# A two-layer encoder on one core: up-products turned weight-stationary, and sums of down weights made ahead through HBM

## The chip, the cores and the metric

The kernel runs on one core of a Trainium2 chip. The metric is the device time in microseconds from start to end; lower is better. The profile is one execution with every instruction recorded.

## What is computed

A trunk of two layers over 256 tokens of width 2048, all in float32. Layer 0 mixes tokens with a bidirectional mLSTM, layer 1 with a bidirectional HGRN2; each mixer is followed by a gated feed-forward block (ConvGLU). The change lies in the feed-forward blocks:

```python
def conv_glu(hn, w_up, conv_w, conv_b, w_down):
    u = hn @ w_up                          # (256, 2048) @ (2048, 2 * 5504)
    a, v = jnp.split(u, 2, axis=-1)
    ...
    c = conv_b
    for j in range(CONV_W):                # width 3 along the tokens
        c = c + ap[:, j:j + s] * conv_w[j]
    return (jax.nn.gelu(c, approximate=False) * v) @ w_down   # (256, 5504) @ (5504, 2048)

for layer in range(DEPTH):
    hn = rmsnorm(h, norm_mix_g[layer])
    h = h + (mlstm_mixer(hn, ...) if layer % 2 == 0 else hgrn_mixer(hn, ...))
    h = h + conv_glu(rmsnorm(h, norm_ffn_g[layer]), ...)
return rmsnorm(h, final_g)
```

## The kernel before

Every matrix product is made of three: activations and weights are each split into a high part (cast to fp32r) and a low remainder, and high x high, high x low and low x high are added up in PSUM. The weights stream from HBM in 1 MB pieces into three buffers tagged `raw`, on SP's queue. `halves` splits a piece: ScalarE casts 1024 columns into `wh`, VectorE subtracts to get `wl` (four buffers each). `split_weights` and `split_pair` are generators of such pieces; `stream` pulls them three ahead of the products that use them.

Three forms of product occur. A `Chunk` of kind `tm` (token-major) holds the activations stationary and streams 512 weight columns, 6 matmuls for each 128 rows of weights. A `Chunk` of kind `fm` (feature-major) holds a weight block stationary: for each 128 rows and each of two 128-column blocks, `wh` against the 512 columns of high and low activations (line 388), then `wl` against the 256 columns of high ones (line 391). With `turns` set, at k = 1 both `wh` passes run first and then both `wl` passes (lines 380 and 382). A `Pair` makes two 512-column output blocks at once, for both halves of the tokens: its unit is a *couple* of two 128-row blocks of weights, which the plan marks by a letter. An `N` couple takes 8 products of three 512-column matmuls; an `S` couple takes 7, as in Strassen's scheme with Winograd's sums, and an `H` is half an `N`. An `S` needs sums of the four weight blocks (`T4`, three subtractions by VectorE, lines 237 to 240), which are split like weights, and sums of the four activation blocks (`forms`, line 399). After the last `S` of a pair, `middle` puts the scheme's accumulators together (`combine`, line 1104) and adds them; `done` adds the rest when the pair is through.

In a feed-forward block the 43 tiles of 128 hidden features are taken in three parts of 16, 16 and 11. For each part, the up products of its tiles run first and then the down products with its features, added into `hm`. Up products go by `Pair`, four tiles of a and v at a time (`UP_PLAN` with three couples of eight by seven; `UP_LAST`, for a part's last group, with two). Their outputs are token-major, so the side job `raise_up` turns each tile by four TensorE transposes (line 1069), convolves, applies Gelu and the gate, splits the result into `g`, and makes the forms that the down pair will need. Down products go by two `Pair`s for each part (`DOWN_PLAN`: two couples of eight by seven for 16 tiles, one for 11); in the last part of layer 1 the second pair is replaced by two `tm` chunks.

The order of the work between matmuls is set by `Side`: side jobs are generators, moved on by `tick` with a written-out estimate of the time that each group of matmuls takes. Within what the dependencies allow, a list scheduler orders the instructions of each engine. A queue is in order once written.

Of the kernel before, what the change touches and what calls it, by code (L numbers as in the profile page):

```python
# [15 lines left out]
P = 128  # L16
T = 256
# [4 lines left out]
GROUP = 4  # L22
UP_PLAN = "SNSNSNNN"
UP_LAST = "SNSNNNNN"
PACE = 2.5
PACE_LAST = 0.8
DOWN_PLAN = {16: "SNSNNNNN", 11: "SNNNNH"}
# [36 lines left out]
def trunk_kernel(ctx, tc, xT, x_d, fg_d, pp_d, cst_d, sel_d, w_gate, w_first, w_aq, w_ak, w_av, w_ao, w_aout,  # L64
                 w_bq, w_bv, w_bg, w_bout, w_up, w_down, w_last, out, mscr):
# [30 lines left out]
    class Side:  # L96
        def __init__(self):
            self.now, self.jobs, self.turned = 0.0, [], False
# [16 lines left out]
        def until(self, ready):  # L115
            while not ready():
                assert self.jobs
                for job in list(self.jobs):
                    self.step(job)

# [102 lines left out]

    def split_pair(ch):
        w, b0 = ch.w, 0
        for kind in ch.plan:
            n = (2 if kind == "H" else 4) * w
            raw = wpool.tile([P, 2048], F32, tag="raw", bufs=RAW, name="raw")
            nc.sync.dma_start(raw[:, :n], ch.src[:, b0:b0 + n])
            b0 += n  # L230
# [4 lines left out]
            T4 = ch.pool().tile([P, 2048], F32, tag="T4", bufs=1, name="T4")  # L235
            b12 = raw[:, 0:w].unsqueeze(1).broadcast_to([P, 2, w])
            dve.tensor_tensor(T4[:, 0:2 * w].rearrange("p (a b) -> p a b", a=2), b12,  # L237
                              raw[:, w:3 * w].rearrange("p (a b) -> p a b", a=2), ALU.subtract)
            dve.tensor_tensor(T4[:, 2 * w:3 * w], raw[:, 2 * w:3 * w], T4[:, 0:w], ALU.subtract)
            dve.tensor_tensor(T4[:, 3 * w:4 * w], raw[:, 3 * w:4 * w], T4[:, 2 * w:3 * w], ALU.subtract)  # L240
# [5 lines left out]
    def stream_pair(ch, take):  # L246
# [18 lines left out]
        left, k = ch.plan.count("S"), 0  # L265
        for c, kind in enumerate(ch.plan):
            end = c == len(ch.plan) - 1
            if kind == "S":
# [3 lines left out]
                F, fin = ch.form(c), left == 0  # L272
# [30 lines left out]
            D = ch.form(c) if left else None  # L303
# [95 lines left out]
    def forms(x2, kind, mp, tag, fe):  # L399

        n = 4 if kind == "S" else 2
        e = fe.tile([P, 512], F32, tag="fe", bufs=1, name="fe")
# [13 lines left out]
    def wanted(plan):  # L416
        last = plan.rfind("S")
        return {c: k for c, k in enumerate(plan) if c <= last}
# [118 lines left out]
    class FinalNorm:  # L537

        def begin(self, mp):
            self.mp = mp  # L540
            self.g = mp.tile([P, D], F32, name="fg")
# [495 lines left out]
    def ffn(layer, norm, nxt):  # L1037
# [5 lines left out]
        def begin():  # L1043
            box["mp"] = stack.enter_context(tc.tile_pool(name="ff", bufs=1))
            box["mp"].tile([P, LEAD], F32, name="lead")
            box["xf"] = tc.tile_pool(name="xf", bufs=1)
            box["xp"] = box["xf"].__enter__()
        norm.pool, norm.temps = lambda: box.get("xp"), lambda: box["mp"]

        def end():  # L1050
            box["xf"].__exit__(None, None, None)
            if last:
                nxt.begin(stack.enter_context(tc.tile_pool(name="fin", bufs=1)))

        def raise_up(st):
            while not st["ready"]:
                yield 0.5
            at, w = st["at"], st["w"]
            mp = box["mp"]
            for j in range(w // P):  # L1060
                f, i = st["f"] + j, st["i"] + j
                if i % 2 == 0:
                    st["GT"].c2 = mp.tile([P, 2, T], F32, tag="c2", bufs=2, name="c2")
                c = st["GT"].c2[:, i % 2]
                pt = aux("pt")
                for n in range(2):
                    for t in range(2):
                        o = n * T + t * P
                        pe.transpose(pt[:, o:o + P], at[:, t, n * 512 + j * P:n * 512 + (j + 1) * P], ident)  # L1069
                cw = [col("conv_w", (layer * 3 + k) * FT + f) for k in range(3)]  # L1070
                act.activation(c, pt[:, 0:T], AF.Identity, scale=cw[1], bias=col("conv_b", layer * FT + f))
                dve.scalar_tensor_tensor(c[:, 1:T], pt[:, 0:T - 1], cw[0], c[:, 1:T], ALU.mult, ALU.add)
                dve.scalar_tensor_tensor(c[:, 0:T - 1], pt[:, 1:T], cw[2], c[:, 0:T - 1], ALU.mult, ALU.add)
                act.activation(c, c, AF.Gelu)
                dve.tensor_tensor(c, c, pt[:, T:2 * T], ALU.mult)
                g = slot(i, "g")
                act.copy(g[:, 0:T], c)
                dve.tensor_tensor(g[:, T:2 * T], c, g[:, 0:T].bitcast(F32), ALU.subtract)
                st["GT"].x[i] = g
                if i % 2 and i // 2 in st["GT"].want:  # L1080
                    st["GT"].forms[i // 2] = forms(st["GT"].c2, st["GT"].want[i // 2], mp, f"gf{i // 2}", mp)
                yield PACE_LAST if st['end'] else PACE
            st["over"] = True

        class Gated:
            def __init__(self, nf):
                self.x, self.forms, self.want = [None] * nf, {}, wanted(DOWN_PLAN[nf])

            def get(self, k):
                side.until(lambda: self.x[k] is not None)  # L1090
                return self.x[k]

            def form(self, c):
                side.until(lambda: c in self.forms)
                return self.forms[c]

        def room(st):
            side.until(lambda: all("over" in o for o in st["wait"]))
            st["at"] = box["mp"].tile([P, 2, 1024], F32, tag="at", bufs=1, name="at")

        def rows(d, w):
            return d.rearrange("p (n c) -> p n c", n=2)[:, :, 0:w]
# [12 lines left out]
        before = None  # L1115
        for part, (f0, nf) in enumerate(PARTS):
            GT = Gated(nf)
            for i in range(0, nf, GROUP):
                w = min(GROUP, nf - i) * P
                st = dict(f=f0 + i, i=i, GT=GT, w=w, end=i + GROUP >= nf, wait=[before] if before else [])  # L1120
                before = st

                def middle(acc, st=st):
                    room(st)
                    at, w, rc = st["at"], st["w"], norm.rc
                    combine(acc, at, w)
                    for t in range(2):
                        v = rows(at[:, t], w)
                        act.activation(v, v, AF.Copy, scale=rc[:, t:t + 1])

                def done(acc, st=st):
                    w = st["w"]
                    plain = "at" not in st
                    if plain:
                        room(st)
                    for t in range(2):
                        d, v, sc = rows(acc["rows"][t], w), rows(st["at"][:, t], w), norm.rc[:, t:t + 1]
                        if plain:
                            act.activation(v, d, AF.Copy, scale=sc)
                        else:  # L1140
                            dve.scalar_tensor_tensor(v, d, sc, v, ALU.mult, ALU.add)
                    st["ready"] = True
                st["ready"] = False
                ch = Pair(w_up[layer, (f0 + i) // GROUP], UP_LAST if i + GROUP >= nf else UP_PLAN, norm.x, norm.form, lambda acc, done=done, st=st: (done(acc), side.push(raise_up(st))),
# [161 lines left out]
```

## Time and profile before

| | |
|---|---|
| median of 3 runs | 2405.66 us (2405.57 to 2408.1) |
| the profiled execution | 2404.82 us, its span 2403.0 us |
| TensorE matmul busy | 2389.1 us, 99% of the span |
| VectorE busy | 2017.9 us, 84% |
| ScalarE busy | 1396.5 us, 58% |
| GpSimd busy | 163.6 us, 7% |
| granted TensorE clock | 0.999 of full speed |
| moved by DMA | 451.01 MB, mean 188 GB/s |

The span runs from the first to the last instruction. A busy share is the time in which the engine had an instruction under way; a busy TensorE need not be at its peak, since matmuls are pipelined and one that takes 0.39 us from start to end is followed by the next after some 0.23. In the profile, PE is TensorE's matmul, PEld its weight load, DVE is VectorE, ACT is ScalarE, POOL is GpSimd and SP the engine that issues the weight DMAs. L255 is line 255 of the kernel. A row of a group of instructions gives count, busy time and mean duration, then the idle time of the engine just before them and what ended it.

### The profile page before, as it was taken

How to read it: one execution, taken by the hardware profiler on the slowest of the kernel's cores; microseconds unless marked ns; L12 is line 12 of the kernel's file. 1: busy time of each engine (PE TensorE's matmuls, PEld its weight loads, DVE VectorE, ACT ScalarE, POOL GpSimd, SP SyncE). 2: the span in 40 equal slices, each digit the busy share in tenths (PEclk: the TensorE clock that was granted, in tenths of full speed). 3: DMA queues.
4: the chain of work that ended last, by engine and by line, in shares of the span. 5: the costliest groups of instructions: out<-in, count | busy, mean ns of one | idle time of the engine just before them, and what ended most of it. 6: DMA issues, size and time to landing. Idle time of an engine off the chain costs nothing.

```text
span 2403.0 us, 34456 instructions
## 1 busy us (share of the span) xinstructions
PE 2389.1 (99%) x13165; PEld 1997.6 (83%) x13165; DVE 2017.9 (84%) x3009; ACT 1396.5 (58%) x2063; POOL 163.6 (7%) x223
## 2 busy tenths in 40 slices
PE   9999999999999999999999999999999999999998
PEld 8888888788887888888888888888878888888897
DVE  7766667998889887997888888886898889988896
ACT  6655465666456555665555555556566556654664
POOL 0100000000000000001222222220000000000000
PEclk9999999999999999999999999999999999999999
DMA  7654554555555556455554555545556555555564
GB/s 295 203 179 170 186 175 175 195 185 198 193 192 193 193 193 210 163 200 182 176 169 167 173 176 168 169 174 178 191 175 210 177 208 193 186 196 195 191 210 143
DMA packets 67061, 451.01 MB, mean 188 GB/s; under 512 B 7744, under 2 KB 8384, under 8 KB 15440
## 3 DMA queue, kind: packets, MB, share of 16 engines
q1 hardware_dynamic: 64800, 442.32, 53.1%
q0 software_dynamic: 1232, 5.31, 1.0%
q8 instruction: 103, 1.69, 0.3%
q10 hardware_dynamic: 864, 1.19, 0.1%
q14 instruction: 62, 0.51, 0.1%
HBM read 446.62 MB, written 2.16 MB: 187 GB/s over the span
## 4 chain that ended last, share of the span: by engine, by line
PE 91%; DVE 7%; issue 1%; ACT 1%; DMA 0%; SPq 0%; POOLq 0%; POOL 0%; ACTq 0%; DVEq 0%
PE c L255 44%; PE mm L388 9%; PE mm L371 7%; PE mm L372 7%; PE mm L373 7%; PE m L255 5%; PE mm L391 4%; DVE wl L162 3%; PE pt L1069 1%; PE mm L380 1%; PE pn L737 1%; PE pd L920 1%; PE py L969 1%; DVE T L237 1%; PE pz L482 0%
## 5 line engine op out<-in xcount | busy, mean ns | idle before, releaser
L161 ACT CAST wh<-raw 128x1024 fp32r<-128x1024 f32 (+1 forms) x837 | 829.1, 1001 | 563.0 <-PE c L255 220.9
L162 DVE TENSOR_TENSOR wl<-raw,wh 128x1024 fp32r<-128x1024 f32 (+1 forms) x837 | 967.5, 1167 | 224.1 <-ACT wh L161 223.3
L255 PE MATMUL c<-wh,xt 128*128 128x512 f32 (+1 forms) x1944 | 620.1, 386 | 0.0
L255 PEld LDWEIGHTS c<-wh,xt 128*128 128x128 f32 x1944 | 363.8, 188 | 71.3 <-ACT wh L161 4.8
L255 PE MATMUL c<-wl,xt 128*128 128x512 f32 (+1 forms) x972 | 374.9, 386 | 0.0
L388 PE MATMUL mm<-xt,wh 128*128 128x512 f32 x940 | 331.9, 396 | 0.0
L255 PE MATMUL c<-wh,g 128*128 128x512 f32 x1028 | 325.3, 390 | 0.0
L161 ACT CAST wh<-T 128x1024 fp32r<-128x1024 f32 (+1 forms) x158 | 161.2, 1038 | 186.7 <-PE c L255 154.6
L391 PE MATMUL mm<-xt,wl 128*128 128x256 f32 x940 | 264.3, 281 | 0.0
L255 PEld LDWEIGHTS c<-wh,g 128*128 128x128 f32 x1028 | 192.8, 188 | 41.2 <-ACT wh L161 1.2
L255 PEld LDWEIGHTS c<-wl,xt 128*128 128x128 f32 x972 | 182.5, 188 | 39.3 <-DVE wl L162 5.1
L162 DVE TENSOR_TENSOR wl<-T,wh 128x1024 fp32r<-128x1024 f32 (+1 forms) x158 | 188.1, 1206 | 31.2 <-ACT wh L161 22.8
L388 PEld LDWEIGHTS mm<-xt,wh 128*128 128x128 f32 x940 | 176.4, 188 | 38.7
L255 PE MATMUL c<-wl,g 128*128 128x512 f32 x514 | 200.8, 391 | 0.0
L255 PE MATMUL c<-wh,F 128*128 128x512 f32 (+1 forms) x500 | 196.0, 395 | 0.8 <-ACT wh L161 0.8
L371 PE MATMUL mm<-wh,xt 128*128 128x512 f32 x480 | 188.2, 392 | 0.0
L372 PE MATMUL mm<-wl,xt 128*128 128x512 f32 x480 | 187.7, 391 | 0.0
L373 PE MATMUL mm<-wh,xt 128*128 128x512 f32 x480 | 187.3, 390 | 0.0
L391 PEld LDWEIGHTS mm<-xt,wl 128*128 128x128 f32 x940 | 177.0, 188 | 0.8
L255 PE MATMUL m<-wh,F 128*128 128x512 f32 (+1 forms) x316 | 116.9, 395 | 0.0
L255 PEld LDWEIGHTS c<-wl,g 128*128 128x128 f32 x514 | 96.5, 188 | 21.3 <-DVE wl L162 1.4
L255 PEld LDWEIGHTS c<-wh,F 128*128 128x128 f32 x500 | 94.0, 188 | 20.2 <-ACT wh L161 1.6
(272 smaller groups left out, 3399.4 us busy)
## 6 DMA issues: line engine op xcount, KB each, us to landing
raw<-in_w_up SPq DMA_DIRECT2D x160, 1024.0 KB, 4.8
raw<-in_w_down SPq DMA_DIRECT2D x79, 1024.0 KB, 4.9
raw<-in_w_bq SPq DMA_DIRECT2D x48, 1024.0 KB, 5.1
raw<-in_w_ao SPq DMA_DIRECT2D x16, 1024.0 KB, 4.8
raw<-in_w_aout SPq DMA_DIRECT2D x16, 1024.0 KB, 4.8
raw<-in_w_bv SPq DMA_DIRECT2D x16, 1024.0 KB, 4.8
raw<-in_w_bg SPq DMA_DIRECT2D x16, 1024.0 KB, 4.8
raw<-in_w_bout SPq DMA_DIRECT2D x16, 1024.0 KB, 4.8
```

The source lines that it names most:

```text
L161: act.copy(wh[:, :m], r)
L162: dve.tensor_tensor(wl[:, :m], r, wh[:, :m].bitcast(F32), ALU.subtract)
L237: dve.tensor_tensor(T4[:, 0:2 * w].rearrange("p (a b) -> p a b", a=2), b12, raw[:, w:3 * w].rearrange("p (a b) -> p a b", a=2), ALU.subtract)
L255: pe.matmul(acc[name][:, 0:w], a, b, start=name not in begun, stop=sp and i == 2)
L371: pe.matmul(ps[t], xh, wh[:, c], start=st, stop=False)
L372: pe.matmul(ps[t], xh, wl[:, c], start=False, stop=False)
L373: pe.matmul(ps[t], xl, wh[:, c], start=False, stop=sp)
L380: pe.matmul(ps[f], wh[:, cs[f]], x, start=st, stop=False)
L388: pe.matmul(ps[f], wh[:, c:c + P], x, start=st, stop=False)
L391: pe.matmul(ps[f][:, 0:T], wl[:, c:c + P], x[:, 0:T], start=False, stop=sp)
L737: pe.matmul(pn[:, 0:258], w, v, start=(i == 0), stop=(i == len(parts) - 1))
L920: pe.matmul(pd[o:o + w, c:c + w], k[:, b * w:(b + 1) * w], q[:, e * w:(e + 1) * w], start=True, stop=True)
```

## The change

- Up products: each tile's a and v is one `fm` chunk of 256 columns (`w_up` is laid out anew for it), normalised by `fm_scaled` and convolved straight from PSUM in `done_up`. There are no couples by seven in the ups any more, no transposes of the result, no `raise_up`, no `at` tile, and no forms of the norm's output. Only the first chunk of each part has `turns`.
- Down pairs: five of eight couples go by seven, and two of five and a half in an 11-tile part (both pairs of a part have the same plan). The letter `P` is an `S` whose weight sums come ready and split from HBM: `split_pair` loads three of its four raw blocks and then the sums, 2 MB in four loads on GpSimd's queue.
- These sums are made by the side job `sums_ahead` during the ups of the same part: two half couples (256 of 512 columns each) for each `P`, one every 12 ticks; load on SP's queue, three subtractions, cast and remainder, then two stores on GpSimd's queue into the new HBM tensor `sums`. Four spare tiles `pr0` to `pr3` serve both the making and the loading.
- The down pair's combining tile now comes from the three `raw` buffers; the last norm's gain tile shares `T4`'s place and is loaded when the last down pair ends.

```diff
-UP_PLAN = "SNSNSNNN"
-UP_LAST = "SNSNNNNN"
-DOWN_PLAN = {16: "SNSNNNNN", 11: "SNNNNH"}
+TURNS = 1
+A = "PSNSPSNN"
+B = "PSNNNH"
+DOWN_PLAN = {16: A, 11: B}
+REST = 8.0
+EACH = 12.0
...
+    def pair_sums(b, t):
+        dve.tensor_tensor(t[:, 0:2], b[:, 0:1].broadcast_to(b[:, 0:2].shape), b[:, 1:3], ALU.subtract)
+        dve.tensor_tensor(t[:, 2], b[:, 2], t[:, 0], ALU.subtract)
+        dve.tensor_tensor(t[:, 3], b[:, 3], t[:, 2], ALU.subtract)
+    def sums_ahead(srcs, box):
+        yield REST
+        due, h = side.now, 256
+        for n, src in srcs:
+            for o in (0, h):
+                while side.now < due and not side.flush:
+                    yield 0.1
+                due += EACH
+                b, t, th, tl = (spare(i, box) for i in range(4))
...
+                nc.sync.dma_start(b, src.rearrange("p (a b) -> p a b", a=4)[:, :, o:o + h])
+                pair_sums(b, t)
+                act.copy(th, t)
+                dve.tensor_tensor(tl, t, th.bitcast(F32), ALU.subtract)
+                for j, v in enumerate((th, tl)):
+                    pool.dma_start(sums[n, j]...[:, :, o:o + h], v...)
+            stored.append(n)
     def split_pair(ch):
...
+            skip = w if kind == "P" else 0
+            nc.sync.dma_start(raw[:, skip:n], ch.src[:, b0 + skip:b0 + n])
+            if kind == "P":
+                yield halves(raw[:, w:3 * w], 2 * w)
+                yield halves(raw[:, 3 * w:4 * w], w)
+                n = ch.made[c]
+                side.until(lambda: n in stored)
+                for i in range(2):
+                    z = [spare(2 * i + j, ch.box) for j in range(2)]
+                    for j in range(2):
+                        pool.dma_start(z[j], sums[n, j][:, 1024 * i:1024 * i + 1024])
+                    yield z
+                continue
...
-        def raise_up(st):
...
+        def done_up(f, i, GT):
+            def go(ps):
...
+                fm_scaled(ps[0], R, a)
+                fm_scaled(ps[1], R, v)
+                act.activation(c, a, AF.Identity, scale=cw[1], bias=col("conv_b", layer * FT + f))
+                dve.scalar_tensor_tensor(c[:, 1:T], a[:, 0:T - 1], cw[0], c[:, 1:T], ALU.mult, ALU.add)
+                dve.scalar_tensor_tensor(c[:, 0:T - 1], a[:, 1:T], cw[2], c[:, 0:T - 1], ALU.mult, ALU.add)
+                act.activation(c, c, AF.Gelu)
+                dve.tensor_tensor(c, c, v, ALU.mult)
+                g = slot(i, "g", mp)
+                act.copy(g[:, 0:T], c)
+                dve.tensor_tensor(g[:, T:2 * T], c, g[:, 0:T].bitcast(F32), ALU.subtract)
...
...
         for part, (f0, nf) in enumerate(PARTS):
-            for i in range(0, nf, GROUP):
-                ch = Pair(w_up[layer, (f0 + i) // GROUP], UP_LAST if i + GROUP >= nf else UP_PLAN, norm.x, norm.form, ..., middle, w=w)
+            for i in range(nf):
+                chunks.append(Chunk("fm", w_up[layer, f0 + i], KT, norm.x, done_up(f0 + i, i, GT), turns=1 if i < TURNS else 0))
+                chunks[-1].apart = bool(part) and i == 0
...
-                    room(before)
-                    combine(acc, before["at"], 512)
+                    at = wpool.tile([P, 2048], F32, tag="raw", bufs=RAW, name="at")...
+                    combine(acc, at, 512)
...
-    n0, n1, n2, n3 = Norm("mix_g", 0), Norm("ffn_g", 0, UP_PLAN), Norm("mix_g", KT), Norm("ffn_g", KT, UP_PLAN)
+    n0, n1, n2, n3 = Norm("mix_g", 0), Norm("ffn_g", 0), Norm("mix_g", KT), Norm("ffn_g", KT)
+    sums = nc.dram_tensor("sums", (count, 2, P, 2048), F32R, kind="Internal").ap()
```

More of the change, by code (lines that the diff above doesn't have):

```diff
@@ L271, in stream_pair @@
                 left -= 1
[L272 removed]
+                F, fin = ch.form(c, kind), left == 0
                 def form(i):
@@ L1089, in get, with form @@
             def get(self, k):
-                side.until(lambda: self.x[k] is not None)
                 return self.x[k]
[L1093 to L1102, printed above, removed]
+            def form(self, c, kind):
+                return self.forms[c, kind]
@@ L1113, in combine @@
                               v5.unsqueeze(1).broadcast_to([P, 2, w]), ALU.add)
-        before = None
         for part, (f0, nf) in enumerate(PARTS):
             GT = Gated(nf)
-            for i in range(0, nf, GROUP):
[L1119 to L1144, printed above, removed]
-                          middle, w=w)
-                ch.pool = lambda: box["mp"]
-                chunks.append(ch)
-            before = dict(wait=[before], over=True)
-            final = last and part == len(PARTS) - 1
@@ L1182, in ffn @@
         return chunks, begin, stack.close
+    numbers = list(range(sums.shape[0]))
     pool.memset(ones, 1.0)
```

130 lines of the change are left out of this document (68 added, 62 removed).

## The prediction

> **What bounds the kernel now.** I read the page first (busy shares, chain), then the two feed-forward stretches cut at their stage boundaries, then in a down stage VectorE's groups and the waits, and the DMA issues last.
>
> ```profile
> span 2403.0 us, 34456 instructions
> PE 2389.1 (99%) x13165; PEld 1997.6 (83%) x13165; DVE 2017.9 (84%) x3009; ACT 1396.5 (58%) x2063; POOL 163.6 (7%) x223
> ...
> DMA  7654554555555556455554555545556555555564
> GB/s 295 203 179 170 186 175 175 195 185 198 193 192 193 193 193 210 163 200 182 176 169 167 173 176 168 169 174 178 191 175 210 177 208 193 186 196 195 191 210 143
> ...
> PE 91%; DVE 7%; issue 1%; ACT 1%; DMA 0%; SPq 0%; POOLq 0%; POOL 0%; ACTq 0%; DVEq 0%
> ```
>
> (The two rows in the middle are the DMA share and the GB/s in 40 slices.) TensorE is 91% of the chain and busy 99% of the span, so a change pays only by shortening TensorE's own stream, and costs wherever the stream is starved. VectorE, at 84%, is next. Stage by stage (columns: stretch, its length, busy time of each engine, clock, DMA share, GB/s), layer 0 and then layer 1; up and down stages alternate, and the last row is layer 1's closing token-major product:
>
> ```profile
> 392.88:569.53 176.65, 175.61 (x797) 143.16 (x795) 160.71 (x209) 112.71 (x151) 1.60 (x1) 1.00 0.54 188
> 569.53:656.18 86.65, 86.65 (x390) 71.17 (x389) 73.47 (x82) 45.61 (x57) 0.00 (x0) 1.00 0.57 200
> 656.18:830.68 174.50, 174.12 (x784) 141.92 (x783) 159.14 (x199) 109.03 (x142) 0.00 (x0) 1.00 0.54 190
> 830.68:917.34 86.66, 86.66 (x389) 71.16 (x388) 73.55 (x82) 45.62 (x57) 0.00 (x0) 1.00 0.57 200
> 917.34:1037.97 120.63, 120.53 (x586) 103.58 (x584) 108.59 (x140) 74.84 (x102) 0.00 (x0) 1.00 0.54 186
> 1037.97:1099.78 61.81, 61.81 (x288) 51.15 (x288) 55.02 (x74) 39.23 (x58) 0.00 (x0) 1.00 0.57 192
> ...
> 1688.47:1865.16 176.69, 175.66 (x796) 143.17 (x795) 160.82 (x209) 112.73 (x151) 1.60 (x1) 1.00 0.54 188
> 1865.16:1951.82 86.66, 86.66 (x389) 71.17 (x388) 73.46 (x82) 45.68 (x57) 0.00 (x0) 1.00 0.58 200
> 1951.82:2126.32 174.50, 174.19 (x784) 141.94 (x783) 159.13 (x199) 109.03 (x142) 0.00 (x0) 1.00 0.55 190
> 2126.32:2212.95 86.63, 86.63 (x390) 71.15 (x388) 73.47 (x82) 45.62 (x57) 0.00 (x0) 1.00 0.57 200
> 2212.95:2333.56 120.61, 120.51 (x586) 103.56 (x584) 108.58 (x140) 74.93 (x102) 0.62 (x1) 1.00 0.56 194
> 2333.56:2364.71 31.15, 31.15 (x145) 25.75 (x144) 26.99 (x33) 18.54 (x25) 0.00 (x0) 1.00 0.56 195
> ```
>
> VectorE is busy 91% of an up stage (159.14 of 174.50) and TensorE still waits for almost nothing there: that is the load this schedule carries. The clock column is 1.00 everywhere, so the clock plays no part.
>
> **Down pairs: the gain.** A couple by seven issues 7 x 3 = 21 matmuls, one by eight 24. A 16-tile pair goes from 2 sevens (186) to 5 (177); an 11-tile pair from one seven (129) to two (126). The 16 or 12 transposes of the last up group, which today run inside each down stage, vanish. What four of them cost:
>
> ```profile
> 712.76 0.40 PE L255 MATMUL c<-wh,xt 128*128 128x512 f32 x1
> 713.00 0.60 PE L1069 MATMUL pt<-cst,at 128*128 128x128 f32 x4
> 713.35 0.47 PE L255 MATMUL c<-wh,xt 128*128 128x512 f32 x1
> 713.67 0.39 PE L255 MATMUL m<-wl,F 128*128 128x512 f32 x1
> 713.90 0.40 PE L255 MATMUL m<-wh,F 128*128 128x512 f32 x1
> ```
>
> Three products fill 712.76 to 713.90, 1.14 us; at the 0.23 us between the last two starts they need 0.69, so four transposes cost about 0.46. A down stage of two pairs is then (86.65 - 4 x 0.46) / 372 = 0.228 us a matmul, boundaries included. After: 2 x 177 x 0.228 = 80.7, which is 5.95 less, four times: -23.8. Layer 0's short stage loses 6 x 0.228 + 3 x 0.46 = 2.75, layer 1's single pair 3 x 0.228 + 3 x 0.46 = 2.05. Downs: -28.6 us.
>
> **Up products: the price.** Weight-stationary means two passes for a weight block, one of 512 columns (wh against xh and xl) and one of 256 (wl against xh); a tile of a and v has 16 x 2 such pairs. No couple by seven is left in the ups. The mLSTM's q and k chunks already run so, two chunks back to back:
>
> ```profile
> 107.06:129.26 22.20, 22.20 (x129) 19.41 (x128) 13.47 (x17) 10.71 (x14) 0.00 (x0) 1.00 0.51 178
> ...
> 1125.67:1135.56 9.89, 9.89 (x59) 8.59 (x57) 8.95 (x14) 6.01 (x10) 6.95 (x9) 1.00 0.48 179
> ```
>
> That is 11.10 us a chunk, 0.347 a pair, against four tiles in 174.50 / 4 = 43.6 today (10.9 a tile, transposes included). Stages become 16 x 11.10 = 177.6 (+3.1), the same plus 2.15 us of norm transposes that the first stage carries today (176.65 - 174.50; +3.1), and 11 x 11.10 = 122.1 (+1.5): +7.7 a layer, +15.4 together. The second row is the bad end: a stretch of the HGRN chunks where 28 pairs (the counts take in neighbours at the edges) took 9.89, 0.353 a pair, 11.30 a tile, with all operands present. It sets in there after a swapped turn of the two passes; the mLSTM chunks, entered from a 512-column stream and turned at k = 1 as every part's first chunk will be, stayed at the good pace. I take 11.10; the bad pace in all 86 tiles costs 86 x 0.20 = +17.
>
> By the Trainium skill's TensorE: Matmul & The Clock Gate, Back-to-back issue gap, the start-to-start of an isolated matmul is N / 2.4 + 2.5 ns, so 216 + 109 = 325 ns a pair, 10.4 us a tile and some 60 us less on 86 tiles. The 0.347 us of the row above disagrees, and the measurement decides.
>
> **VectorE, the likeliest place for a new bound.** From a down stage:
>
> ```profile
> L162 DVE TENSOR_TENSOR wl<-raw,wh 128x1024 fp32r<-128x1024 f32 x28 | 33.7, 1220 | 5.0 <-ACT wh L161 5.0
> L162 DVE TENSOR_TENSOR wl<-T,wh 128x1024 fp32r<-128x1024 f32 x8 | 9.6, 1220 | 1.7 <-ACT wh L161 1.7
> L237 DVE TENSOR_TENSOR T<-raw 128x1024 f32<-128x1024 f32 x4 | 4.9, 1220 | 0.2 <-DMA raw<-in_w_down 0.2
> L1156 DVE TENSOR_TENSOR hx<-hx,at 128x1024 f32<-128x1024 f32 x4 | 4.7, 1220 | 0.0
> L1161 DVE TENSOR_TENSOR hx<-hx,c 128x1024 f32<-128x1024 f32 x3 | 3.7, 1221 | 4.7 <-PE c L255 4.7
> L239 DVE TENSOR_TENSOR T<-raw,T 128x512 f32<-128x512 f32 x4 | 2.7, 687 | 0.0
> ```
>
> Durations overlap: count times mean over these and the smaller groups comes to about 79 us, while the busy column above has 73.47 for 82 operations, so one occupies some 0.07 less: 1.15 for 1024 columns, 0.62 for 512. An S couple then takes 3 x 1.15 + 0.62 for splits and 1.15 + 2 x 0.62 for sums, 6.5; a P couple 1.15 + 0.62 = 1.8, since its sums come split from memory; an N couple 2.3. Plan PSNSPSNN: 3 x 6.5 + 2 x 1.8 + 3 x 2.3 = 30.0, plus combining (2 x 0.62 + 3 x 1.15 = 4.7) and closing (2.3): 37 of a pair's 40.35 us, 92%. In the ups a tile needs 4 splits (4.6), some 10 short operations (about 3.5), its share of the forms (0.5) and of the sums made ahead (8 halves of 2.4 over 16 tiles, 1.2): 9.8 of 11.1, 88%. Both are about the 91% carried today, so VectorE is costed at nothing; without its lead of up to four split pieces, each S couple's excess over TensorE's 4.8 us (1.7) would show.
>
> **Sums by way of HBM.** For each P: two half loads on SP's queue, four stores on POOL's (two for each half) and later four loads on POOL's; 19 P couples in all (4 for each long part, 2 and 1 for the short ones). POOL has nothing else in the up and down stages (0 to 1.60 busy above), so only landing counts:
>
> ```profile
> raw<-in_w_down SPq DMA_DIRECT2D x79, 1024.0 KB, 4.9
> ...
> hx<-in_x POOLq DMA_DIRECT2D x2, 1024.0 KB, 9.6
> ```
>
> The first P of a part is loaded during the ups. The second P of a pair has its buffers free after 4.8 us and its sums needed at about 21; the next pair's first has from 24.5 to 42. The two 1 MB loads on POOL's queue took 9.6 us each side by side, in the busiest slice, so a P's 2 MB need about 10 of 16 or 17 us: hidden. Traffic in the downs rises from 200 to about 12.1 MB / 40.3 us = 300 GB/s, and the first slice of the page ran at 295.
>
> SP's half loads wait for a spare tile released one 12-tick interval earlier; behind them on SP queue the raw weights, three buffers deep. Costed at nothing for that; but the combining tile now also takes one of those three, for some 8 us late in each pair, when a raw lands in 4.9 us and is needed every 5. I take 0.2 us for each of 11 pairs, +2, between nothing and the wait's full 1.3 (+14).
>
> **Up to down.** The down pair needs the last up chunk's PSUM buffer at its fourth product, 3 x 3 x 0.228 = 2.05 us in. It is read by two copies and two adds (0.37 and 0.42 each by the next rows, with a multiplication between), behind at most one 1.1 us operation: 1.6 to 2.8 us after the chunk's end, so -0.4 (nothing) to +0.8 each. I take 0.4, six times: +2.4. The way from a down pair to the next ups uses other banks, as now.
>
> ```profile
> L423 DVE TENSOR_TENSOR qk<-mm,b 128x256 f32<-128x256 f32 x2 | 0.8, 418 | 0.0
> L422 ACT COPY b<-mm 128x256 f32<-128x256 f32 x2 | 0.7, 366 | 0.0
> ```
>
> The norm's combinations for the ups go (off the path: ScalarE and VectorE work in the projections), and the final gain's load moves from the start of the last down pair to its end, where a 30 us product stage covers it. Both nothing.
>
> **Sum.** The profiled execution took 2404.8 us (2403.0 span, 1.8 around it), 0.85 under the median 2405.7. 2404.8 - 28.6 + 15.4 + 2.0 + 2.4 = 2396.0.
>
> **The rivals.**
> 1. The ups run at the bad pace: 2396 + 17 = 2413, slower. For it: the 9.89 us row. Against: three mLSTM stretches and the start of the HGRN's kept the good one. It decides from 11.2 us a tile (8.8 us lost over 86).
> 2. VectorE becomes the bound in the downs, slower: it cannot hold the splits ahead when it must stand and wait for a pair's last product (4.7 us over 3 waits above, up to 2.3 each). One full wait exposed in each of 8 long pairs is +19: 2415. It decides at 1.1 us a pair. Against it: those waits exist today at 85% busy with no stall of TensorE.
> 3. The sums or raw weights come late: 1 us for each of six second P couples or pairs leaves 2402, no change; 2400 to 2406. For it: 300 GB/s on queues that interleave. The Trainium skill, SBUF — State Buffer, SBUF: two separate sides, says that DMAs from POOL's queue starve for descriptors while VectorE runs a two-port operation; nearly all VectorE work here is two-input, at one element a cycle or so (1024 in 1.22 us), so no row here shows it.
> 4. The 256-column pass costs half a 512-column one, 1.5 x 0.228 = 0.342 a pair and 10.94 a tile: 86 x 0.16 = 14 less, 2382. The mLSTM row speaks against it, at 0.347. The Trainium skill's gap, quoted above, is the far end of the same idea.
>
> **How the numbers follow.** Forecast 0.57, with its own range 2389 to 2400; rival 1, 0.12; rival 2, 0.11; rival 3, 0.17; rival 4, 0.03. The range leaves out rival 4 and the far ends of 1 and 2: from 2387 (both allowances at nothing, and a first up stage that sheds more than its norm work) to 2412. About 0.2%, 4.8 us, is what a measurement of this kernel can tell from no change. Faster: the forecast, rival 4 and the mildest of rival 3, 0.62. Same: the rest of rival 3 and a bad pace in some parts, 0.21. Slower: most of 1 and 2, 0.17.
>
> **What would show it.** Right: up stages of 177 to 180 and 122 us, down stages near 81 and 59, no transposes of line 1069's kind, VectorE near 90% in the downs, 19 x 4 loads of sums landing within 10 us. Wrong: up pairs at 0.353; TensorE's weight loads waiting for wl in the downs by microseconds, or for the spare tiles; gaps at each part's change from up to down.

## The result, and the profile after

The changed kernel takes 2431.35 us (median; 2426.1 to 2437.75) against 2405.61 (2405.54 to 2408.1) of the kernel before in the same session: a ratio of 1.0106, 95% interval 1.0078 to 1.0133. It is slower by 1.1%; the prediction was 2396.0 with a range of 2387 to 2412. The profiled execution took 2437.75 us, the longest of the four runs; its span is 2435.7.

The page of the changed kernel, span, TensorE, and the chain that ended last by engine and by line:

```profile
span 2435.7 us, 37196 instructions
PE 2398.5 (98%) x14200; PEld 2044.1 (84%) x14200; DVE 1937.7 (80%) x3159; ACT 1335.2 (55%) x2057; POOL 256.6 (11%) x375
...
PE 80%; DMA 7%; DVE 6%; issue 4%; ACT 1%; POOL 0%; SPq 0%; POOLq 0%; ACTq 0%; DVEq 0%
PE mm L436 32%; PE mm L439 16%; PE mm L420 6%; PE mm L419 6%; PE mm L421 6%; PE c L302 6%; DVE wl L167 3%; DMA sums<-pr 3%; PE m L302 2%; DMA raw<-in_w_down 2%; DMA raw<-in_w_up 1%; ACT wh L166 1%; PE mm L428 1%; PE pn L785 1%; PE pd L968 1%
```

TensorE was 91% of the chain before and is 80% now. Transfers went from 0 to 7%, and the stores of the sums (`sums<-pr`) alone are 3%. By stages the loss is easier to place. Before, the two projections ahead of the feed-forward blocks (columns as in the prediction's table):

```profile
299.95:392.88 92.93, 92.93 (x436) 77.46 (x435) 59.33 (x92) 52.46 (x89) 1.34 (x2) 1.00 0.52 181
1593.72:1688.47 94.75, 94.75 (x549) 79.14 (x548) 65.69 (x116) 54.81 (x97) 1.39 (x2) 1.00 0.54 187
```

After, projection, then up and down stages in turn, layer 0 and layer 1 (the last row, here and in the prediction's table, is layer 1's single down pair):

```profile
300.49:400.54 100.05, 95.85 (x435) 79.06 (x434) 70.56 (x102) 55.06 (x82) 13.34 (x20) 0.97 0.90 284
400.54:579.40 178.86, 178.86 (x1037) 156.61 (x1036) 137.22 (x227) 100.13 (x154) 2.75 (x4) 1.00 0.60 204
579.40:660.89 81.49, 80.84 (x357) 66.29 (x355) 72.51 (x83) 44.27 (x54) 7.85 (x14) 1.00 0.76 263
660.89:845.86 184.97, 180.66 (x1025) 156.84 (x1024) 150.32 (x245) 102.95 (x152) 12.09 (x18) 0.99 0.81 265
845.86:927.45 81.59, 80.88 (x357) 66.29 (x355) 72.45 (x83) 44.29 (x54) 7.78 (x14) 1.00 0.76 264
927.45:1049.89 122.44, 122.44 (x706) 107.34 (x704) 97.53 (x152) 67.57 (x99) 6.42 (x10) 1.00 0.78 263
1049.89:1113.06 63.17, 61.37 (x270) 49.80 (x269) 50.28 (x68) 35.85 (x54) 2.12 (x4) 0.97 0.54 199
...
1607.21:1712.09 104.88, 98.61 (x550) 81.17 (x548) 73.14 (x121) 55.87 (x89) 10.69 (x15) 0.97 0.79 255
1712.09:1894.15 182.06, 182.06 (x1037) 158.12 (x1036) 140.35 (x231) 100.28 (x155) 4.99 (x8) 1.00 0.63 215
1894.15:1976.01 81.86, 80.89 (x357) 66.29 (x355) 72.63 (x83) 44.40 (x54) 7.78 (x14) 1.00 0.75 262
1976.01:2163.89 187.88, 182.60 (x1025) 157.71 (x1024) 150.13 (x245) 102.29 (x152) 12.10 (x18) 0.99 0.80 261
2163.89:2244.95 81.06, 80.83 (x356) 66.30 (x355) 72.55 (x83) 44.26 (x54) 7.78 (x14) 1.00 0.75 264
2244.95:2368.23 123.28, 122.40 (x706) 106.64 (x704) 94.17 (x144) 65.71 (x97) 3.58 (x6) 1.00 0.69 235
2368.23:2396.81 28.58, 28.58 (x128) 23.65 (x127) 22.98 (x28) 15.98 (x21) 0.53 (x1) 1.00 0.60 218
```

The long downs are where the prediction put them (81.1 to 81.9). Two things are not. The projections, in which no line changed, take 7.1 and 10.1 us more and have GpSimd at work on 20 and 15 instructions instead of 2. And the second up stages take 185 and 188 us instead of 177.6, with TensorE idle for 4 to 5 us and the clock at 0.99.

Where the projections' time went: SP's queue there (start, length, engine, line, transfer, count).

```profile
321.28 0.38 SPq L253 DMA_DIRECT2D pr<-in_w_down  x1
322.54 6.31 SPq L157 DMA_DIRECT2D raw<-in_w_aout  x2
328.95 0.41 SPq L253 DMA_DIRECT2D pr<-in_w_down  x1
338.20 0.33 SPq L157 DMA_DIRECT2D raw<-in_w_aout  x1
342.54 0.38 SPq L253 DMA_DIRECT2D pr<-in_w_down  x1
```

These half loads belong to the first part's sums and were to come one every 12 ticks during the ups, which begin at 400. A half load depends on nothing but a free spare tile, so the list scheduler placed it as early as its own timing had one: all eight halves of a first part stand in the projection. What they do to the other queues shows in the waits (engine, line, waited for: us in total, times, longest):

```profile
DVE pr L257 <- DMA sums<-pr: 59.8, 14, 9.1
ACT pr L256 <- DMA sums<-pr: 54.3, 13, 10.2
```

and, in one case from the second up stage, in the chain (start, us, what), with the rows of TensorE around it:

```profile
708.39 17.03 DMA sums<-pr
...
725.51 0.09 DVE pr L257
725.61 1.05 issue
726.66 1.23 DVE wl L167
...
727.93 0.39 PE mm L439
```

```profile
723.67 0.39 PE L436 MATMUL mm<-xt,wh 128*128 128x512 f32 x1
727.93 0.39 PE L439 MATMUL mm<-xt,wl 128*128 128x256 f32 x1 [3.86 <-DVE wl L167]
...
728.86 0.63 PE L436 MATMUL mm<-xt,wh 128*128 128x512 f32 x1
729.29 0.41 PE L439 MATMUL mm<-xt,wl 128*128 128x256 f32 x1
729.50 0.63 PE L436 MATMUL mm<-xt,wh 128*128 128x512 f32 x1
```

A store of half a couple took 17.03 us to land. The next half's remainder (line 257) writes the tile that this store reads, so VectorE stood at it; behind it in the same queue stood the weight remainder (line 167) that TensorE needed: a gap of 4.26 us. After the gap the matmuls start 0.43 and 0.21 us apart, half their pace, for some 3 us more. In median a store lands in 8.3 us, and both kinds of sums transfers move 512 KB:

```profile
sums<-pr POOLq DMA_DIRECT2D x76, 512.0 KB, 8.3
pr<-sums POOLq DMA_DIRECT2D x76, 512.0 KB, 7.9
```

**Theory A**: the sums cost through the in-order queues. Casts and subtractions that wait for a store or a half load stand ahead of weight casts. **Rival B**: the added traffic itself makes weight loads late, wherever it is put. **C**: TensorE's pace in the up stages, which came out at 0.347 us a pair of matmuls in some and 0.353 in others, has a cause of its own.

### The profile page after: what moved, and what is told of

Its sections match the earlier page's. It is cut to its first block, busy times and chain, and to the rows that moved or that the text cites. A ratio compares the mean times of both kernels' runs of the same rounds, so it can differ in the third digit from the quotient of the medians.

```text
span 2435.7 us, 37196 instructions
## 1 busy us (share of the span) xinstructions
PE 2398.5 (98%) x14200; PEld 2044.1 (84%) x14200; DVE 1937.7 (80%) x3159; ACT 1335.2 (55%) x2057; POOL 256.6 (11%) x375
## 4 chain that ended last, share of the span: by engine, by line
PE 80%; DMA 7%; DVE 6%; issue 4%; ACT 1%; POOL 0%; SPq 0%; POOLq 0%; ACTq 0%; DVEq 0%
PE mm L436 32%; PE mm L439 16%; PE mm L420 6%; PE mm L419 6%; PE mm L421 6%; PE c L302 6%; DVE wl L167 3%; DMA sums<-pr 3%; PE m L302 2%; DMA raw<-in_w_down 2%; DMA raw<-in_w_up 1%; ACT wh L166 1%; PE mm L428 1%; PE pn L785 1%; PE pd L968 1%
## 5 line engine op out<-in xcount | busy, mean ns | idle before, releaser
L436 PE MATMUL mm<-xt,wh 128*128 128x512 f32 x3678 | 1291.4, 396 | 1.8 <-ACT wh L166 1.8
L439 PE MATMUL mm<-xt,wl 128*128 128x256 f32 x3678 | 1026.4, 280 | 8.7 <-DVE wl L167 8.7
L436 PEld LDWEIGHTS mm<-xt,wh 128*128 128x128 f32 x3678 | 690.6, 188 | 162.2 <-ACT wh L166 3.4
L439 PEld LDWEIGHTS mm<-xt,wl 128*128 128x128 f32 x3678 | 694.2, 189 | 12.5 <-DVE wl L167 10.1
L302 PE MATMUL c<-wh,g 128*128 128x512 f32 x666 | 218.0, 390 | 0.0
L302 PEld LDWEIGHTS c<-wh,g 128*128 128x128 f32 x666 | 125.3, 188 | 26.1
L302 PE MATMUL c<-wl,g 128*128 128x512 f32 x333 | 130.0, 390 | 0.0
L421 PEld LDWEIGHTS mm<-wh,xt 128*128 128x128 f32 x480 | 90.2, 188 | 18.5
L419 PEld LDWEIGHTS mm<-wh,xt 128*128 128x128 f32 x480 | 90.1, 188 | 18.4
L420 PEld LDWEIGHTS mm<-wl,xt 128*128 128x128 f32 x480 | 90.1, 188 | 17.3
L257 DVE TENSOR_TENSOR pr<-pr,pr 128x1024 fp32r<-128x1024 f32 x38 | 46.4, 1222 | 72.1 <-DMA sums<-pr 59.8
L471 ACT COPY b<-mm 128x256 f32<-128x256 f32 x236 | 86.4, 366 | 14.3 <-DVE z L472 6.7
L256 ACT CAST pr<-pr 128x1024 fp32r<-128x1024 f32 x38 | 39.9, 1051 | 77.7 <-DMA sums<-pr 54.3
```

The lines of the kernel that those rows point to most:

```text
L257: dve.tensor_tensor(tl, t, th.bitcast(F32), ALU.subtract)
L302: pe.matmul(acc[name][:, 0:w], a, b, start=name not in begun, stop=sp and i == 2)
L419: pe.matmul(ps[t], xh, wh[:, c], start=st, stop=False)
L420: pe.matmul(ps[t], xh, wl[:, c], start=False, stop=False)
L421: pe.matmul(ps[t], xl, wh[:, c], start=False, stop=sp)
L436: pe.matmul(ps[f], wh[:, c:c + P], x, start=st, stop=False)
```

## The experiments

Each is compared with the kernel before, run beside it (2405.8 to 2406.4 us in all). Stage times are from the profiled executions; wide_rows spread from 2412.0 to 2432.1, and its profiled execution is the shortest, while that of late_load (2428.94 us) is the longest of its four.

| kernel | time, us | ratio, 95% interval | span | projections | ups of layer 0 | ups of layer 1 |
|---|---|---|---|---|---|---|
| no_sums | 2432.75 | 1.0112 [1.0097, 1.0127] | 2430.2 | 92.9, 94.8 | 178.9, 180.8, 124.3 | 178.8, 180.8, 124.3 |
| late_load | 2420.62 | 1.0069 [1.0053, 1.0085] | 2426.9 | 92.9, 94.8 | 186.1, 186.2, 122.1 | 184.7, 184.5, 122.1 |
| more_spares | 2412.57 | 1.0028 [1.0017, 1.0039] | 2413.5 | 94.5, 97.6 | 178.9, 182.2, 124.2 | 183.0, 177.7, 122.4 |
| wide_rows | 2421.71 | 1.0068 [1.0041, 1.0094] | 2410.2 | 92.9, 100.2 | 178.9, 179.9, 122.1 | 178.9, 180.8, 122.1 |
| split_load | 2400.86 | 0.9975 [0.9965, 0.9984] | 2399.6 | 92.9, 94.8 | 178.9, 177.5, 122.1 | 178.8, 177.5, 122.1 |
| split_only | 2399.33 | 0.9969 [0.9956, 0.9981] | 2398.6 | 92.9, 94.8 | 178.9, 177.5, 122.1 | 179.2, 177.5, 122.1 |
| spares_rows | 2414.59 | 1.0035 [1.0024, 1.0046] | 2410.3 | 95.1, 102.0 | 178.9, 177.8, 123.2 | 181.1, 178.1, 122.3 |
| no_turn | 2421.83 | 1.0064 [1.0050, 1.0077] | 2420.5 | 92.9, 94.8 | 178.9, 177.6, 122.1 | 178.9, 177.6, 122.1 |
| split_best | 2395.67 | 0.9955 [0.9943, 0.9968] | 2394.0 | 92.9, 94.8 | 178.9, 177.5, 122.1 | 178.8, 177.5, 122.1 |
| split_best1 | 2396.90 | 0.9963 [0.9950, 0.9977] | 2395.1 | 92.9, 94.8 | 181.6, 177.5, 122.1 | 178.8, 177.5, 122.1 |
| sums_pinned | 2398.32 | 0.9967 [0.9954, 0.9979] | 2396.4 | 92.9, 94.8 | 178.9, 179.1, 122.1 | 178.8, 177.5, 122.1 |
| best_no_turn | 2406.84 | 1.0005 [0.9996, 1.0014] | 2404.6 | 92.9, 94.8 | 178.9, 180.8, 124.3 | 178.9, 180.8, 124.3 |

**no_sums: the new ups alone.**

```diff
-A = "PSNSPSNN"
-B = "PSNNNH"
+A = "SNSNNNNN"
+B = "SNNNNH"
```

> The changed kernel with the old down plans (SNSNNNNN and SNNNNH): no couple has its sums made ahead, nothing is stored in HBM or loaded from it; the weight-stationary ups stay. Theory A (the loss is ScalarE and VectorE standing in queue order at the cast or the remainder of a half, because the stores of the half before still hold its single spare tiles): both projection stages ahead of the feed-forward blocks fall back to about 93 and 95 us, the second parts' ups to 177.6 to 181; total 2404.8 - 10.1 (transposes) + 15.4 (ups) + up to 8 for boundaries and a slow pace in one part = 2411 to 2419. Rival B (the added DMA traffic delays the weights) says the same here. Rival C (the loss belongs to the weight-stationary ups themselves): the second parts' ups stay at 185 to 188, total above 2430.

Measured: 2432.75 us, a miss, no faster than the changed kernel. The projections are back at 92.93 and 94.77 and no up stage stalls, so those losses come with the sums. But two costs appear that do not come from the sums. The second and third up stages run at 0.353 us a pair without any stall (rows with no_turn, below), some 10.7 us in four stages. And the downs gain nothing from the vanished transposes: 86.3 us against 86.65.

**late_load, more_spares, wide_rows: one remedy each.** late_load fixes the half load in SP's order behind the weight load written before it:

```diff
-                nc.sync.dma_start(b, src.rearrange(...)[:, :, o:o + h])
+                late(b, src.rearrange(...)[:, :, o:o + h])
```

> The load of each half is pinned in SP's order behind the weight load traced before it, so that the sums of the first part are made in its ups at the written 12 ticks and no longer in the projection ahead of them. Theory A: the projections return to about 93 and 95 us (-17), and at one half in 12.8 us against stores that land in 8.3 us in the median fewer halves stand: 2405 to 2418. Rival B: the same bytes pass during a stage just as full, the stalls move into the first ups and the total stays at 2424 to 2438.

more_spares makes the remainder in the place of the sums and takes two sets of tiles in turn:

```diff
-                b, t, th, tl = (spare(i, box) for i in range(4))
+                b, tl, th = (spare(i, box) for i in ((0, 1, 2), (0, 3, 4))[half % 2])
+                t, half = tl, half + 1
```

> Two sets of spare tiles in turn for the high part and the remainder (the remainder is written in the place of the sums, five tiles in all), so that a half waits for the stores of the half before last. Traffic and order as in the change. Theory A: ScalarE's and VectorE's waits for the stores (54 and 60 us) nearly vanish, the projections come to 93 to 96 us and the second ups to 178 to 181: 2400 to 2412. Rival B: no change, 2424 to 2438, with the projections at 98 to 105 us.

wide_rows stores a half as one block with rows of 4 KB instead of 1 KB pieces, and gathers when it loads:

```diff
-                    pool.dma_start(sums[n, j].rearrange("p (a b) -> p a b", a=4)[:, :, o:o + h], ...)
+                    pool.dma_start(sums[n, j, o // h], v)
```

> Each half is stored whole, in rows of 4 KB instead of four rows of 1 KB for each partition; the loads then gather rows of 1 KB. The same bytes. Theory A, in the form that a store of many small packets takes turns with the 8 KB packets of the weights and so lands late: stores land in 5 us or less instead of 8.3, ScalarE and VectorE stand for half as long, 2408 to 2422; the loads of the sums take longer to land, without being waited for. Rival B: no change, 2424 to 2438.

Each moved or lessened the loss without removing it. late_load missed both of its ranges; wide_rows came into its first one without the faster stores that were the reason for it, and more_spares ended just above its own. late_load gave the projections back (92.93 and 94.77), and its long ups rose to 184 to 186 us: VectorE now stood at the first subtraction for the half load, since the scheduler placed that right behind the load.

```profile
DVE pr L230 <- DMA pr<-in_w_down: 74.6, 36, 3.9
```

more_spares took nearly all of VectorE's and ScalarE's waits for stores away (from 59.8 and 54.3 us to the row below) and gained most of the three, though its stores landed in 11.3 us:

```profile
DVE pr L230 <- DMA sums<-pr: 12.9, 3, 6.4
```

wide_rows did not shorten the landing (8.4 us in median against 8.3) and the two waits only fell, to 35.1 and 28.8 us. So wait and landing time are not the same thing: what counts is who stands at the store, and for how long after it was issued.

**split_load, split_only, spares_rows: pace by the engine's own order.** In split_load and split_only the load is fixed as in late_load, and the subtractions are fixed in VectorE's order 9 ticks later, so a half's load, sums and stores are spread over its 12 ticks. split_load has two sets of tiles and whole rows beside that; spares_rows has these two without the fixing.

```diff
+LAG = 9.0
...
+                late(b, ...)
+                while side.now < due - EACH + LAG and not side.flush:
+                    yield 0.1
+                pair_sums(b, t, tc.keep_in_program_order)
```

> Two pairs of spare tiles in turn, halves stored whole in rows of 4 KB, the half's load pinned behind the weight load traced before it, and its subtractions pinned on VectorE 9 of the written ticks later. Theory A (the late stores and the early half loads, through the in-order queues of ScalarE, VectorE and SyncE, are what the sums cost): projections ahead of the FFN 92.9 and 94.8 us as before, ups 178 to 181, 178 to 181 and 122 to 124, long downs near 81.6; span 2396 to 2404, a time about 2398 to 2406, within 0.3% of the kernel before. Rival B (the added traffic itself slows the weight loads, wherever it is put): ups keep stalls of 4 to 9 us a long stage, span 2412 or more.

> As split_load, but with the single set of spare tiles and stores in rows of 1 KB: only the pins are added. Theory A: projections 92.9 and 94.8; a half comes every 12 ticks and a store lands in 8 us (median) to 17, so most casts find their tile free: ups 178 to 182, span 2400 to 2412. If the casts still stand for stores (VectorE and ScalarE waiting for them 30 us or more in sum), the tiles and the rows are needed beside the pins, and the span is above 2415. Rival B: as for split_load, 2412 or more, with those waits gone.

> Two pairs of spare tiles and whole rows of 4 KB, no pin: half loads go where the scheduler puts them, into the projections ahead of the first parts too. Theory A: waits for stores under 10 us in sum, projections within 2 us of 92.9 and 94.8, span 2402 to 2411, below more_spares (2413.5). Rival B: no better than more_spares.

split_load and split_only are faster than the kernel before, by 0.25% and 0.31%, their ups free of stalls but for 0.4 us in one stage; split_only came out a little below its range. split_only moves the same bytes by the same transfers as the changed kernel, and its stores land no sooner (8.8 us), yet VectorE and ScalarE stand for them 10.2 and 3.3 us in sum instead of 59.8 and 54.3:

```profile
DVE pr L260 <- DMA sums<-pr: 10.2, 7, 4.9
ACT pr L259 <- DMA sums<-pr: 3.3, 1, 3.3
```

Rival B falls for the projections and the ups. spares_rows (span 2410.3) is in its range but not below more_spares in the median: without the fixed order the projections still pay 2.2 and 7.2 us, more than expected.

**no_turn: the pace.** no_sums with `TURNS = 0`.

> no_sums (the down plans of before, no sums by way of HBM) without the swapped order of four matmuls at the second k of each part's first tile. Theory C (the swapped turn is what puts a stage at 353.3 ns a pair of matmuls where it is not at 346.7): second and third parts at 346.7, ups 178.9, 177.7 and 122.2, span 2419 to 2421 against 2430.2 of no_sums. Rival (the pace is set by what stands ahead of the stage, not by the turn): paces as in no_sums, 2428 to 2432. If the turn toggles it, the first parts go to 353.3 as well: 2426 to 2428.

The second up stage of layer 0 in no_sums, no_turn and, for later, best_no_turn and split_best:

```profile
658.41:839.22 180.81, 180.81 (x1025) 156.74 (x1024) 130.12 (x201) 94.34 (x143) 0.00 (x0) 1.00 0.57 189
```

```profile
659.45:837.04 177.59, 177.59 (x1026) 155.26 (x1024) 130.16 (x201) 94.98 (x143) 0.00 (x0) 1.00 0.58 192
```

```profile
653.97:834.80 180.83, 180.83 (x1025) 156.92 (x1024) 151.90 (x248) 103.31 (x153) 13.66 (x20) 1.00 0.86 274
```

```profile
653.51:831.05 177.54, 177.54 (x1025) 155.24 (x1024) 151.63 (x248) 103.69 (x153) 13.61 (x20) 1.00 0.87 278
```

TensorE is busy throughout in all four, at full clock. In no_turn all stages are good, as theory C expected; leaving out a swap of four matmuls saved 9.7 us of span.

**split_best, split_best1, sums_pinned: which remedy does what.** split_best is split_load with whole rows only in the part of 11 tiles; split_best1 is the same with the single set of tiles; sums_pinned is split_only without the `late` on the load, so that only SP's order differs from it.

> split_load with whole rows of 4 KB in HBM only in the part of 11 tiles; the long parts store 1 KB pieces and load the sums in rows of 4 KB again, with two pairs of spare tiles. Expected, if the layout sets what the downs wait for: long downs near 81.4 us as in split_only (not 82 to 84.6 as in split_load, where TensorE stood up to 2.8 us for the sums' loads), the third down of layer 0 near 59.4 as in split_load (not 63.8 as in split_only, where weight loads landed in 8.7 us beside 512 KB sums loads); ups 178.9, 177.5, 122.1; span 2394 to 2396, time 2395 to 2397. If the spare tiles rather than the rows made the third down short or the long ones long, 2398 to 2402.

> As split_best with the single set of spare tiles of the changed kernel, so split_only with whole rows in the part of 11 tiles. If the rows alone decide: third down of layer 0 near 59.4 us, span 2394 to 2396; if the second pair of spare tiles does: 63.8 as in split_only, span about 2398.6.

> split_only without the pin on the half's load: VectorE, ScalarE, TensorE and GpSimd have the same order as in split_only, and only SyncE's order differs (the half loads stand some weight loads earlier, the first one inside nothing but the ups). Theory A by VectorE and ScalarE (what costs is the subtraction, cast or remainder that stands ahead of weight casts): no stall comes back, span 2397 to 2401 like split_only (2398.6). Rival by SyncE (a half load that waits for its spare tile holds the weight loads queued behind it, the step that the prediction costed at nothing): weights late again, span 2406 or more.

sums_pinned keeps all the gain (span 2396.4, just below its range) although its first half load stands behind the sixth of the projection's 16 weight loads, and not, as in split_only, behind the fourth of the ups'. (Its expectation has that load in the ups, which is wrong.) What had to be fixed is VectorE's order; SyncE's half loads then come later by themselves, since their spare tiles come free later (of layer 0's first eight, one still stands in the projection). Fixing SyncE's order alone, in late_load, did not do it. split_best reaches 2395.67 us, 0.45% under the kernel before; split_best1 is level with it but for a stall of 2.8 us in its first up stage. The size of the packets goes with the third down of layer 0: 63.8 us in split_only, 59.5 and 59.6 in split_best1 and split_best. In a stretch from the down's start, first split_only, then split_load (59.4 us), the queue's packets and MB, and KB each and median us to landing:

```profile
q0 software_dynamic: 576, 2.10, 16.0%
...
raw<-in_w_down SPq DMA_DIRECT2D x5, 1024.0 KB, 8.7
pr<-sums POOLq DMA_DIRECT2D x4, 512.0 KB, 7.3
```

```profile
q0 software_dynamic: 2176, 2.10, 21.1%
...
raw<-in_w_down SPq DMA_DIRECT2D x5, 1024.0 KB, 6.2
pr<-sums POOLq DMA_DIRECT2D x8, 256.0 KB, 9.8
```

With the 2.10 MB in packets of 3.6 KB in the mean (2.10 MB / 576) the weights landed in 8.7 us; with packets of about 1 KB they landed in 6.2 and the sums were later. The Trainium skill, DMA: Bandwidth & Descriptors, Queues, rings and completion order, says that an engine takes the queues in turn packet by packet; these rows agree, if a packet is what the profile counts. Packet size is not all of it: sums_pinned has the large packets too, yet there the weights land in 6.7 us and the down takes 60.2. In the four other kernels with large packets it takes 63.2 to 64.2, in the six with small ones 59.1 to 59.6. In the long downs it is the other way about: there the sums are what comes late (81.9 to 84.6 us in split_load; 81.3 to 82.1 in split_best, which has the same tiles and larger packets).

**best_no_turn: does the turn set the pace?** split_best with `TURNS = 0`.

> split_best without the swapped order of four matmuls in each part's first tile. If leaving the turn out is by itself enough for the good pace, as no_turn suggests: all six up stages at 0.347 us a pair again (178.9, 177.6, 122.1), span within 1 us of split_best (2394.0). If the pace is set by how the stage is entered, some stage without the turn goes to 0.353: its 16 tiles take 3.2 us more, 11 tiles 2.2, span 2396 or more.

The four stages that are good in split_best are all bad here (the third and fourth row above): 10.6 us of span. With the old down plans the turn made these stages slow, with the new ones it makes them fast; the two first stages take 178.8 to 178.9 us with and without it.

The traces show why. Near the start of a second or third up stage the list scheduler puts four matmuls into the turn's order (two `wh` passes, then two `wl`) on its own (lines 436 and 439 in no_sums and no_turn). One such swap in no_turn, the stretches of its stage before and behind it, and last the stretch behind the same swap in no_sums (the counts take in neighbours at the edges):

```profile
665.09 0.63 PE L436 MATMUL mm<-xt,wh 128*128 128x512 f32 x2
665.56 0.39 PE L439 MATMUL mm<-xt,wl 128*128 128x256 f32 x2
...
659.45:665.10 5.65, 5.65 (x34) 4.91 (x33) 4.72 (x4) 2.57 (x3) 0.00 (x0) 1.00 0.39 115
665.80:837.04 171.24, 171.24 (x991) 149.74 (x989) 125.44 (x197) 91.78 (x140) 0.00 (x0) 1.00 0.58 194
...
664.70:839.22 174.52, 174.52 (x990) 151.25 (x989) 125.40 (x197) 91.13 (x140) 0.00 (x0) 1.00 0.57 191
```

In no_turn 16 pairs ahead of the swap take 0.353 us each (5.65 / 16) and 494 pairs behind it 0.347. In no_sums the turn has already brought 0.347, and the same swap brings 0.353 back (174.52 / 494). In all the second and third stages of the four kernels, each swap behind the first four matmuls changes the pace: one in no_turn and three in split_best end good, two in no_sums and in best_no_turn end bad. So the turn is one flip among several, and behind the first four matmuls the scheduler added one with the old down plans and two with the new. In the first stages the norm's transposes stand between the matmuls of the first tile; behind them the pace is 0.347 in these four kernels, with the turn or without it.

## Why the prediction was wrong

Each term in us against the profile before. The changed kernel's ups are divided by what split_best, which has no stalls, shows of them, and by the tiles at 0.353 (some 32 by the starts of their matmuls, at the 0.20 that a bad stage shows: (180.81 - 177.59) / 16); the rest is stalls. They are at the high end, since this execution took 6.4 us more than the median.

| | predicted | changed kernel | split_best |
|---|---|---|---|
| ups, their own passes, with the wait of the down's first products | +15.4 + 2.4 | +13.3 | +13.3 |
| ups at the bad pace | 0 | +6.4 | 0 |
| stalls in the ups | 0 | +16.2 | 0 |
| projections | 0 | +17.2 | 0 |
| downs, combining tile included | -28.6 + 2.0 | -21.8 | -24.3 |
| the rest | 0 | +1.4 | +2.0 |
| sum | -8.8 | +32.7 | -9.0 |

- **The step that failed** is "Sums by way of HBM": "SP's half loads wait for a spare tile released one 12-tick interval earlier", "costed at nothing". It took the written 12 ticks for the order on the chip and looked at SP's queue alone. The half loads came earlier than written, and the queues that had to be costed were VectorE's and ScalarE's, where the cast and remainder wait for a store of 8 us in median and up to 17. That is the stalls and the projections, 33.4 us; with VectorE's order fixed, sums_pinned has 1.5 us of stalls left and none of the projections' loss. Rival 3 named the right place and put 2400 to 2406 on it, with the price of one microsecond for each late load. The landing of the stores, for which the next half waits, was not priced at all.
- **The ups' price was right**: 178.8 to 178.9, 177.5 and 122.1 us where they are undisturbed, against 179.75, 177.6 and 122.1. The wait of the down's first products for the last up chunk (+2.4) was not seen as a cost on top.
- **Rival 1 happened in parts.** The prediction held against it that the mLSTM's chunks are turned and good, and for it that the HGRN's bad pace sets in after a turn. Both rows were read as if the turn or the entry set the pace; each swap flips the pace, and the scheduler adds swaps of its own, so a turn proves neither. In the changed kernel the stage at 1712 is bad from near the end of its first tile on, the second stages in part.
- **The downs' matmuls were right**: 354 in two pairs, 81.1 to 81.9 us long where 80.7 was said, the remainder a gap of about 1 us where the second pair begins. The transposes' 1.84 us are saved where a `P` opens the pair. In no_turn and no_sums, where an `S` still opens it, the gap that they had covered shows instead:

```profile
576.48 0.39 PE L302 MATMUL c<-wh,g 128*128 128x512 f32 x1
578.10 0.50 PE L302 MATMUL c<-wl,g 128*128 128x512 f32 x1 [1.23 <-DVE wl L167]
```

  The short down of layer 0 was mis-sized: 63.17 us (+1.4) against a saving of 2.75, with weights that land late beside the sums and the clock at 0.97. With 1 KB pieces on the load (split_best) it is 59.64, a saving of 2.2.
- **VectorE is not the bound** (rival 2): it is 89% busy in the long downs (72.51 of 81.49) where 92% was worked out, and TensorE keeps up. Rival 4 did not occur.

Once VectorE's order is fixed and the short part's rows are chosen, the sum holds: 2395.67 measured (split_best), 2396.0 predicted. That it agrees so closely is luck in part, since the downs save 2.3 less than said, the ups cost 4.5 less, and the rest adds 2.0.

What stays open is why the order of four matmuls changes the pace of all that follow, why a stall sometimes does so too, and why the stage at 1712 went bad near the end of its first tile, behind the norm's transposes.

## What to carry to other kernels

An interval that is written into a program is not an interval on the chip: work that depends on nothing is placed by the scheduler, so its place on every engine must be looked up or fixed. When a side job shares an engine with the critical stream, cost the longest wait of each of its instructions there, the landing of its own stores included, and order it so late that what it needs has come by then. A term that goes may have covered a wait: look at what stood beside it before counting it as saved.

## What the runs showed of the hardware

- A pair of matmuls against 512 and 256 columns runs at one of two steady paces, 0.347 or 0.353 us, with all operands present and the clock at 1.00. A swapped order of four matmuls changes from one to the other, in either direction, and the new pace lasts to the end of the stage: 177.54 and 180.83 us for the same stage.
- A 512 KB store on GpSimd's queue, issued at 708.39, took 17.03 us to land beside the weight stream.
- After the 4.26 us gap TensorE ran at half pace from 728.86 on (0.43 us and 0.21 us start to start) but not in the first microsecond after it. The Trainium skill, TensorE: Matmul & The Clock Gate, Part 1, says that the clock halves when TensorE was idle through a window of about 3.4 us, and that these windows run freely; the half pace and its late onset agree. The length does not: in the same run half pace followed 3.10 us of idle time (matmuls again from 2008.36), and in more_spares 2.29 us (again from 1712.11, half pace from 1712.68).
